# The v projection of the first 128 rows taken from un-normalised rows laid out by feature, with four matmuls on a tile of ones during the first loads

## The chip, the cores and the metric

The kernel runs on one core of one Trainium2 chip. A core has five engines that each work through a list of their own in order: TensorE for matmuls (PE in the profile; PEld is its loading of weights), VectorE (DVE), ScalarE (ACT), GpSimd (POOL) and SyncE (SP), which here issues the DMA transfers. They meet at semaphores. The metric is the device time of one launch in microseconds (us); lower is better. One profiled execution also leaves a trace, in which every instruction has a start and a duration.

## The reference

The reference is one inference step of a four-layer streaming encoder in float32. 640 rows of width 1024 go through it: 512 of a new stream and 128 of running streams. The change touches only the beginning of the first layer:

```python
def rms_norm(x, g):
    y = xf * lax.rsqrt(jnp.mean(xf * xf, axis=-1, keepdims=True) + EPS)
    return (y * g.astype(jnp.float32)).astype(x.dtype)
...
def chunk_mlp(u, v, v_gain, w_s, b_s):
    mu = jnp.mean(vf, axis=-1, keepdims=True)
    var = jnp.mean(jnp.square(vf - mu), axis=-1, keepdims=True)
    vn = ((vf - mu) * lax.rsqrt(var + EPS) * v_gain.astype(jnp.float32)).astype(v.dtype)
...
hp = rms_norm(xp, norm_mix_pre[layer])
proj = h @ w_in
u, v, bg, cg, xb = jnp.split(proj, ...)
```

A row `h` is `x * r * g`, where `r` is one number for the row and `g` one number for each feature. `v` is a product of `h` with 512 columns of `w_in`, and is then normalised over its 512 columns again.

## The kernel before

The 640 rows are five tiles of 128 rows (`t` = 0 to 4). The head of the program, up to the first units of the even mixer, does this:

- `main` queues the loads on SP's list: row tile 0, the gain `X.gain` (one row of 1024 numbers sent to all partitions), two of the four weight pieces of the v projection, row tile 1, the other two pieces. Row tiles 2 to 4 follow later. Every one of these transfers is 512 KB.
- `pre_norm` makes the norm of a row tile: ACT squares and sums it, DVE adds EPS, POOL takes the power -0.5 (the helper `rsqrt`), and DVE multiplies row, `r` and gain in one instruction. PE then transposes the tile in eight 128x128 steps into two PSUM banks (the helper `flip`), and `X.take` splits the result.
- A split (the helper `split`) writes a float32 value as a high part, made by ACT, and a low part, made by DVE as the difference. A product then takes three matmuls: high by high, high by low, low by high. The four weight pieces are split in the same way by `operand`.
- `Quarters` holds the transposed rows for later in seven tiles `x` (tag X), two tiles `a21` and two float32 copies `f`. `take` writes the splits (`x_93`, `x_94` and so on in the lists below) and copies of both banks to `f`. The tiles `a21` and `f` come from the pool `hidp`, which has seven buffers.
- `v_proj` makes 24 matmuls of 128x512 for each row tile: eight steps `k` over the features, three matmuls each, into one PSUM bank. `v_evac` then takes mean and variance of the bank on DVE, a power -0.5 on POOL, and writes the normalised tile `vn` on ACT. Three more `hidp` tiles hold `vn`.
- PSUM has eight banks, shared by transposes and products through the pool `psp`. A bank is free again when its last reader is done.
- The units of the mixer follow (`Units`, products of 128x320 from x and q tiles).

The order is set in two steps. `Weave` runs the generators against a clock of its own, which counts the matmuls issued; `pre_norm` of tile `t` is spawned with a wait of `A1 + (t - 1) * A2`, here 2000 and 5000. The Tile framework then arranges the instructions of each engine; `tc.high_priority()` moves the norms ahead, and while `Ordered.on` is set, ACT and DVE keep the program's order. What comes out is a fixed list for each engine.

Of the kernel before, what the change touches and what calls it, by code (L numbers as in the profile page):

```python
# [8 lines left out]
F32 = mybir.dt.float32  # L9
F32R = mybir.dt.float32r  # L10
AF = mybir.ActivationFunctionType
ALU = mybir.AluOpType
AX = mybir.AxisListType

P = 128
D = 1024
NK = D // P
# [8 lines left out]
HK = NK // 2  # L26
FT = 22
EPS = 1e-6
# [7 lines left out]
A1 = 2000  # L36
A2 = 5000
# [68 lines left out]
def trunk_kernel(  # L106
# [26 lines left out]
    c_w,  # L133
    c_scale,
    rb_rev,
    yp,
    ys,
    ncp,
# [9 lines left out]
    nc = tc.nc  # L148
    act, dve = Ordered(tc, nc.scalar), Ordered(tc, nc.vector)

    cst = ctx.enter_context(tc.tile_pool(name="cst", bufs=1))
# [3 lines left out]
    hidp = ctx.enter_context(tc.tile_pool(name="hidp", bufs=7))  # L155
# [6 lines left out]
    W = Weave()  # L162
# [6 lines left out]
    def flip(out, in_):  # L169
        W.now += 109  # L170
        nc.tensor.transpose(out=out, in_=in_, identity=ident)  # L171
# [3 lines left out]
    def nm(s):  # L175
        uid[0] += 1
        return f"{s}{uid[0]}"

    def bank(shape=(P, 512)):
        return psp.tile(list(shape), F32, tag="ps", name=nm("ps"))  # L180

    def t4(shape):
        return t4p.tile(list(shape), F32, tag="t4", name=nm("t4_"))

    def t2(shape):
        return t2p.tile(list(shape), F32, tag="t2", name=nm("t2_"))

    def st(n=1):
        return stp.tile([P, n], F32, tag="st", name=nm("st"))
# [8 lines left out]
    def bcast(src, n, alloc):  # L198
        g = alloc([P, n])
        nc.sync.dma_start(out=g, in_=src.partition_broadcast(P))  # L200
        return g

    def x10(shape, dtype=F32):
        return xpool.tile(list(shape), dtype, tag="X", name=nm("x"))

# [13 lines left out]
    def operand(src):  # L219
        n = src.shape[-1]  # L220
        q = qp.tile([P, 2, D], F32R, tag="q", name=nm("q"))
        split((q[:, 0, :n], q[:, 1, :n]), src)
        return q
# [4 lines left out]
    def split(dst, val):  # L228
        act.copy(out=dst[0], in_=val)
        dve.tensor_tensor(out=dst[1], in0=val, in1=dst[0].bitcast(F32), op=ALU.subtract)  # L230

    def rsqrt(ms):
        r = st()
        nc.gpsimd.tensor_tensor(out=r, in0=ms, in1=mhalf, op=ALU.pow)  # L234
        return r
# [113 lines left out]
                split((self.s4[:, 0, :, o], self.s4[:, 1, :, o]), s4)  # L349
                W.signal(self.sum[t], 4500)  # L350

    def pre_norm(t, x, X, wait, xn=None):
        if xn is None:
            xn = t4([P, D])
        with tc.high_priority():
            norm = Norm()
            norm.add(x, xn)
            r = norm.get()
            dve.scalar_tensor_tensor(out=xn, in0=x, scalar=r, in1=X.gain, op0=ALU.mult, op1=ALU.mult)
        yield wait  # L360
        ps = []
        for half in range(2):
            ps.append(bank((P, HK, P)))
            for i in range(HK):
                k = HK * half + i
                flip(ps[half][:, i, :], xn[:, k * P : (k + 1) * P])
        yield 500
        X.take(t, ps)

# [29 lines left out]
    def group_cols(g):  # L399
        return slice(0, GA) if g == 0 else slice(GA, NT)  # L400

    def wst(X, hl, g):
        for t in ((0, 1), (2, 3, 4))[g]:
            yield X.ev[t]
        cols = group_cols(g)
# [9 lines left out]
                yield  # L415
        return ps[:, :n]

    def v_proj(X, hls, evac):
        for t in range(TT):
            for e in X.ready(t):  # L420
                yield e
            ps = bank()
            for k in range(NK):
                q = hls[k // 2][:, :, k % 2 * 512 : (k % 2 + 1) * 512]
                x = X.rows(k, t)
                mm(ps, x[0], q[:, 0, :], k == 0, False, 512)
                mm(ps, x[0], q[:, 1, :], False, False, 512)
                mm(ps, x[1], q[:, 0, :], False, k == NK - 1, 512)
                if k % 4 == 3:
                    yield  # L430
            evac(t, ps)
# [50 lines left out]
    def in_row(t):  # L482
        return xp[t * P : (t + 1) * P, :] if t < 4 else xs
# [224 lines left out]
        o = hist_n + NP  # L708
        return buf[:, o : o + NB * (hist_n + LS)].rearrange("p (b s) -> p b s", s=hist_n + LS)

    def even_mixer(X, hls):
        vn = {}
        vns = [hidp.tile([P, 2, NT], F32, tag="hid", name=nm("vn")) for _ in range(3)]
        consts = [t4([P, 2, 512]) for _ in range(2)]
# [2 lines left out]
        def v_evac(t, ps):  # L717
            stats = st(6)
            dve.bn_stats(out=stats, in_=ps)
            mv = st(2)  # L720
            dve.bn_aggr(out=mv, in_=stats)
            ve = st()
            dve.tensor_scalar(out=ve, in0=mv[:, 1:2], scalar1=EPS, scalar2=None, op0=ALU.add)
            r = rsqrt(ve)
            vn[t] = vns[t // 2][:, t % 2, :512]
            nm_ = st()
            dve.scalar_tensor_tensor(
                out=nm_, in0=mv[:, 0:1], scalar=-1.0, in1=r, op0=ALU.mult, op1=ALU.mult
            )
            act.activation(out=vn[t], in_=ps, func=AF.Identity, scale=r, bias=nm_)  # L730
            if t == 4:
                o = t2([P, 512])
                dve.tensor_tensor(out=o, in0=vn[t], in1=gn, op=ALU.mult)
                nc.sync.dma_start(out=nav, in_=o)
# [1 line left out]
        gn = bcast(v_gain[0], 512, lambda _: consts[0][:, 0, :])  # L736
        gcol = cst.tile([P, 4], F32, name="gcol")
        nc.sync.dma_start(out=gcol, in_=v_gain_t)
        yield from v_proj(X, hls, v_evac)
        W.signal(v_ready, 4000)  # L740

        wT = consts[1][:, 0, :].rearrange("p (g i) -> p g i", i=P)
# [3 lines left out]
        for b in range(NB):  # L746
            r = slice(b * LS, (b + 1) * LS)
            nc.sync.dma_start(out=wS[r, :, r], in_=sp_wT[0:LS, :, 0:LS])
        for g in range(4):
            for w in (wT, wS):  # L750
                nc.gpsimd.affine_select(  # L751
                    out=w[:, g, :],
                    in_=w[:, g, :],
# [510 lines left out]
    def main():  # L1264
        X = Quarters(None, True)
        feed = fetch([ev_v[i] for i in range(4)])
        xt = []

        def load(t):
            xt.append(t4([P, D]))  # L1270
            nc.sync.dma_start(out=xt[t], in_=in_row(t))

        def start(t, wait):
            g = pre_norm(t, xt[t], X, wait)
            next(g)
            W.spawn(g, 0, wait)

        Ordered.on = True
        load(0)
        X.gain = bcast(g_mix_pre[0], D, t4)  # L1280
        w = [next(feed) for _ in range(2)]
        load(1)
        w += [next(feed) for _ in range(2)]
        first = pre_norm(0, xt[0], X, 0)
        next(first)
        hls = [operand(w[0])]
        for _ in first:
            pass
        W.signal(X.top[0])
        hls.append(operand(w[1]))  # L1290
        start(1, A1)
        hls += [operand(w[2]), operand(w[3])]
        for t in range(2, TT):
            load(t)
            start(t, A1 + (t - 1) * A2)
        Ordered.on = False
        X = yield from even_mixer(X, hls)
        nxt = []

        def mid():  # L1300
            gpost = bcast(g_ffn_post[0], D, t4)
            nxt.append(Normed(bcast(g_mix_pre[1], D, t4)))
            return make_fin(gpost, x_row, x_row, nxt[0])

        yield from ffn(0, X, mid)
        X = yield from odd_mixer(nxt[0])

        def end():
            gpost = bcast(g_ffn_post[1], D, t4)
            return make_fin(gpost, x_row, y_row, None)  # L1310

        yield from ffn(1, X, end)
# [97 lines left out]
```

## Time and profile before

| | |
|---|---|
| median of 3 runs | 1320.55 us (1320.53 to 1320.88) |
| the profiled execution: its time | 1320.24 us |
| its span, first to last instruction | 1318.5 us |
| DVE busy | 889.0 us (67%) |
| ACT busy | 614.0 us (47%) |
| POOL busy | 54.9 us (4%) |
| matmuls recorded | 8060 |
| moved by DMA | 150.12 MB, mean 114 GB/s |

Times in a timeline are counted from the span's start. A timeline's row has the start, the busy time, the engine, the source line, the operation with its output and input tiles and their shape, the number of instructions merged into the row, and in brackets the idle time ahead of it with what ended that. Helpers record many operations, so many rows carry line 99 (the wrapper around ACT and DVE) or 167 (the helper `mm`), and the tile names tell them apart.

### The profile page before, as it was taken

Reading aid. Unit: us, or ns where it says so; the run is one execution under the profiler, and the core shown is the slowest. Engines: PE = TensorE matmul, PEld = TensorE weight load, DVE = VectorE, ACT = ScalarE, POOL = GpSimd, SP = SyncE. Lnnn points to the kernel's source line nnn. Section 1 sums busy time; section 2 is a strip of 40 time slices with the busy share of each in tenths; the row PEclk is TensorE's granted clock in tenths of the full one; section 3 lists DMA queues with packets and bytes.
Section 4 is the critical chain, followed back from the end, with each engine's and each line's share of the span. In section 5 each row is a group of like instructions: output and inputs, shape, how many; then the busy total and the mean of one; then the engine's idle time right before and its main releaser. Section 6 shows DMA issues by size and latency. Waiting matters only on the chain.

```text
span 1318.5 us, 20069 instructions
## 1 busy us (share of the span) xinstructions
PE 1294.0 (98%) x8060; PEld 1178.4 (89%) x8060; DVE 889.0 (67%) x1452; ACT 614.0 (47%) x1130; POOL 54.9 (4%) x107
## 2 busy tenths in 40 slices
PE   6999999999999999999999999999999999999997
PEld 5998989989899998998799885789999898998996
DVE  6985779837576675776736556489557575864766
ACT  5644546535254352454433455366455261551551
POOL 2200101000000000000210000010000000000000
PEclk9999999999999999999999999999999999999999
DMA  7212253212223122126435336532213021230233
GB/s 249 73 65 81 96 200 138 96 48 81 96 73 120 53 77 112 64 84 218 163 120 195 147 143 250 197 128 102 107 64 128 32 98 63 96 115 30 97 128 128
DMA packets 45965, 150.12 MB, mean 114 GB/s; under 512 B 6576, under 2 KB 8496, under 8 KB 45872
## 3 DMA queue, kind: packets, MB, share of 16 engines
q1 hardware_dynamic: 45872, 148.84, 31.2%
q8 instruction: 63, 1.03, 0.3%
q14 instruction: 30, 0.25, 0.1%
HBM read 133.57 MB, written 15.26 MB: 113 GB/s over the span
## 4 chain that ended last, share of the span: by engine, by line
PE 86%; DVE 5%; issue 3%; ACT 2%; DMA 2%; POOL 1%; SPq 0%; DVEq 0%; POOLq 0%; ACTq 0%
PE ps L167 84%; DVE t L99 3%; PE ps L171 1%; DMA xbuf<-t 1%; POOL st L234 1%; ACT t L99 1%; DMA raw<-in_dram 1%; DVE q L99 1%; ACT q L99 1%; DVE x L99 1%; DVE st L99 0%; ACT ps L99 0%; ACT f L99 0%; POOL t L751 0%; SPq L380 0%
## 5 line engine op out<-in xcount | busy, mean ns | idle before, releaser
L167 PE MATMUL ps<-x,q 128*128 128x320 f32 (+2 forms) x4884 | 727.4, 309 | 1.2 <-DVE q L99 0.8
L167 PEld LDWEIGHTS ps<-x,q 128*128 128x128 f32 x4884 | 717.5, 188 | 6.2 <-issue 2.9
L167 PE MATMUL ps<-q,hid 128*128 128x512 f32 x1800 | 417.3, 391 | 0.2 <-DVE hid L99 0.2
L99 ACT CAST q<-raw 128x1024 fp32r<-128x1024 f32 (+1 forms) x278 | 269.7, 977 | 296.8 <-PE ps L167 247.1
L99 DVE TENSOR_TENSOR q<-raw,q 128x1024 fp32r<-128x1024 f32 (+1 forms) x278 | 313.9, 1132 | 134.4 <-ACT q L99 129.3
L167 PEld LDWEIGHTS ps<-q,hid 128*128 128x128 f32 x1800 | 335.5, 188 | 70.9 <-issue 1.7
L99 ACT COPY t<-ps 128x320 f32<-128x320 f32 (+2 forms) x304 | 135.0, 451 | 193.7 <-PE ps L167 173.8
L99 DVE TENSOR_TENSOR t<-ps,t 128x512 f32<-128x512 f32 (+2 forms) x164 | 100.3, 614 | 93.2 <-PE ps L167 93.0
L99 DVE TENSOR_TENSOR raw<-raw 128x512 f32<-128x512 f32 (+1 forms) x141 | 121.9, 866 | 11.6 <-DMA raw<-in_dram 10.0
L99 DVE TENSOR_TENSOR t<-t,t 128x512 f32<-128x512 f32 (+4 forms) x107 | 57.8, 551 | 48.5 <-ACT t L99 46.7
L234 POOL TENSOR_TENSOR st<-st,mhalf 128x1 f32<-128x1 f32 x45 | 31.7, 705 | 1005.9 <-DVE st L99 1001.1
L99 DVE SCALAR_TENSOR_TENSOR t<-t,st,t 128x512 f32<-128x512 f32 (+1 forms) x60 | 54.5, 925 | 16.6 <-POOL st L234 15.1
L99 ACT ACTIVATE t<-t 128x320 f32<-128x320 f32 (+1 forms) x60 | 40.1, 668 | 45.0 <-issue 26.2
L171 PE MATMUL ps<-ident,t 128*128 128x128 f32 x288 | 42.2, 281 | 12.0 <-DVE t L99 9.6
L171 PEld LDWEIGHTS ps<-ident,t 128*128 128x128 f32 x288 | 33.4, 143 | 21.9 <-DVE t L99 9.9
L99 ACT CAST hid<-t 128x320 fp32r<-128x320 f32 (+1 forms) x96 | 45.9, 482 | 11.1 <-DVE t L99 8.9
L99 DVE TENSOR_TENSOR t<-t 128x320 f32<-128x320 f32 (+3 forms) x90 | 48.8, 542 | 1.4
L99 DVE TENSOR_TENSOR hid<-t,hid 128x320 fp32r<-128x320 f32 (+1 forms) x96 | 48.8, 512 | 0.1
L167 PE MATMUL ps<-q,x 128*128 128x512 f32 x192 | 47.6, 402 | 1.2 <-DVE st L99 0.8
L99 ACT ACTIVATE ps<-t 128x512 f32<-128x512 f32 x40 | 24.1, 603 | 50.6 <-DVE t L99 50.6
L167 PEld LDWEIGHTS ps<-q,x 128*128 128x128 f32 x192 | 36.1, 192 | 10.6 <-DVE q L99 2.3
L99 DVE TENSOR_TENSOR t<-t,ps 128x320 f32<-128x320 f32 x47 | 22.9, 487 | 33.2 <-PE ps L167 33.2
(90 smaller groups left out, 497.5 us busy)
## 6 DMA issues: line engine op xcount, KB each, us to landing
raw<-in_dram SPq DMA_DIRECT2D x184, 512.0 KB, 4.1
x<-in_dram SPq DMA_DIRECT2D x24, 512.0 KB, 6.1
t<-in_dram SPq DMA_DIRECT2D x22, 512.0 KB, 5.8
xbuf<-t SPq DMA_DIRECT2D x15, 512.0 KB, 3.4
t<-xbuf SPq DMA_DIRECT2D x15, 512.0 KB, 3.9
out_dram<-t SPq DMA_DIRECT2D x15, 256.0 KB, 2.0
c<-in_dram SPq DMA_DIRECT2D x4, 512.0 KB, 4.2
fscr<-x SPq DMA_DIRECT2D x2, 768.0 KB, 3.3
```

The source lines that it names most:

```text
L99: ins = op(*args, **kw)
L167: nc.tensor.matmul(out, lhsT=lhsT, rhs=rhs, start=start, stop=stop, skip_group_check=more)
L171: nc.tensor.transpose(out=out, in_=in_, identity=ident)
L234: nc.gpsimd.tensor_tensor(out=r, in0=ms, in1=mhalf, op=ALU.pow)
```

## The change

Row tile 0 is loaded twice. The host lays out the first 128 rows by feature (`first_t`: 128 features, eight groups, 128 rows), and the gain in the same way (`first_g`). Two loads of 256 KB bring `first_t`; DVE multiplies the first half by the gain and POOL the second; ACT and DVE split the halves into two new `hidp` tiles `top`. The v projection of tile 0 takes these, and so does not wait for tile 0's norm. The factor `r` of the row, which it lacks, is put in afterwards: `v_evac` of tile 0 multiplies the variance by `r` twice and the scale by `r` once (two more instructions of 128x1). The row-wise tile 0 is still loaded, normed, transposed and kept, for the units.

The order of the loads becomes: first half of `first_t`, `first_g`, two weight pieces, second half of `first_t`, row tile 1, two weight pieces, the gain row, row tile 0. Tile 1 is normed ahead of tile 0, and the waits of the spawns are new. Ahead of all this DVE writes a tile of ones, and four float32 matmuls of 128x512 multiply it by itself into a bank that nobody reads.

```diff
-    def pre_norm(t, x, X, wait, xn=None):
+    def pre_norm(t, x, X, wait, xn=None, scale=None, pause=False):
...
             r = norm.get()
+            if scale is not None:
+                scale.append(r)
+        if pause:
+            yield
+        with tc.high_priority():
             dve.scalar_tensor_tensor(out=xn, in0=x, scalar=r, in1=X.gain, op0=ALU.mult, op1=ALU.mult)
...
-    def v_proj(X, hls, evac):
+    def v_proj(X, hls, evac, first=None):
         for t in range(TT):
-            for e in X.ready(t):
-                yield e
+            if t or first is None:
+                for e in X.ready(t):
+                    yield e
...
+                    x = [f[:, k, :] for f in first]
...
+            var = mv[:, 1:2]
+            if t == 0:
+                var = st()
+                dve.tensor_scalar(
+                    out=var, in0=mv[:, 1:2], scalar1=scale[0], scalar2=scale[0], op0=ALU.mult, op1=ALU.mult
+                )
             ve = st()
-            dve.tensor_scalar(out=ve, in0=mv[:, 1:2], scalar1=EPS, scalar2=None, op0=ALU.add)
+            dve.tensor_scalar(out=ve, in0=var, scalar1=EPS, scalar2=None, op0=ALU.add)
             r = rsqrt(ve)
+            if t == 0:
+                own, r = r, st()
+                dve.tensor_tensor(out=r, in0=own, in1=scale[0], op=ALU.mult)
...
-        load(0)
-        X.gain = bcast(g_mix_pre[0], D, t4)
-        w = [next(feed) for _ in range(2)]
+        ones = t2([P, 512])
+        dve.memset(ones, 1.0)
+        ps = bank()
+        for _ in range(4):
+            nc.tensor.matmul(ps, lhsT=ones[:, :P], rhs=ones, start=True, stop=True)
+        gt = cst.tile([P, NK], F32, name="gt")
+        xt0 = t4([P, NK, P])
+        nc.sync.dma_start(out=xt0[:, :HK], in_=first_t[:, :HK])
+        nc.sync.dma_start(out=gt, in_=first_g)
+        w = [next(feed)]
+        nc.sync.dma_start(out=xt0[:, HK:], in_=first_t[:, HK:])
+        w.append(next(feed))
+        xt.append(None)
         load(1)
         w += [next(feed) for _ in range(2)]
-        first = pre_norm(0, xt[0], X, 0)
+        X.gain = bcast(g_mix_pre[0], D, t4)
+        xt[0] = t4([P, D])
+        nc.sync.dma_start(out=xt[0], in_=in_row(0))
+        top = [hidp.tile([P, NK, P], F32R, tag="hid", name=nm("top")) for _ in range(2)]
+        hls = []
+        for i in range(2):
+            c = slice(i * HK, (i + 1) * HK)
+            (nc.gpsimd if i else dve).tensor_tensor(
+                out=xt0[:, c], in0=xt0[:, c], in1=gt[:, c].unsqueeze(2).broadcast_to([P, HK, P]), op=ALU.mult
+            )
+        for i in range(2):
+            c = slice(i * HK, (i + 1) * HK)
+            split((top[0][:, c], top[1][:, c]), xt0[:, c])
+            hls.append(operand(w[i]))
+        second = pre_norm(1, xt[1], X, A1 + 3000, pause=True)
+        next(second)
+        hls += [operand(w[2]), operand(w[3])]
+        next(second)
+        W.spawn(second, 0, A1 + 3000)
+        scale = []
+        first = pre_norm(0, xt[0], X, 0, None, scale)
         next(first)
...
+        W.spawn(first, 0, 2 * A2 - 500)
         for t in range(2, TT):
             load(t)
-            start(t, A1 + (t - 1) * A2)
+            start(t, A1 + t * A2 - 500)
```

The change moves instructions on all engines in the head. Three places are shown: PE and ACT from the end of row tile 1's v projection to the start of tile 2's, and DVE where the units' first weights are split. The lists name a tile with its number; `[waits ...]` names the engines or DMA queues whose semaphore a row waits for.

On PE before, `ps_291` is the v product of row tile 1, `ps_316` and `ps_321` the transposes of row tile 3, and `ps_337` the v product of row tile 2 (its transposed rows are in `q_92`):

```order
L167 MATMUL ps_291<-q_154,x_94 128x512 x3
L167 MATMUL ps_291<-q_157,x_94 128x512 x6
L171 MATMUL ps_316<-ident,t_38_172 128x128 [waits DVE_49,PE_49]
L171 MATMUL ps_316<-ident,t_38_172 128x128 x3
L171 MATMUL ps_321<-ident,t_38_172 128x128 [waits PE_49]
L171 MATMUL ps_321<-ident,t_38_172 128x128 x3
L167 MATMUL ps_337<-q_124,q_92 128x512 [waits Activation_49]
L167 MATMUL ps_337<-q_124,q_92 128x512 x5
```

On PE now, `ps_258` is the v product of row tile 1, `ps_281` and `ps_286` the transposes of row tile 2, `ps_351` and `ps_356` those of row tile 3, and `ps_382` the v product of row tile 2:

```order
L173 MATMUL ps_281<-ident,t_36_166 128x128 x3
L173 MATMUL ps_286<-ident,t_36_166 128x128 [waits PE_49]
L173 MATMUL ps_286<-ident,t_36_166 128x128 x3
L169 MATMUL ps_258<-q_149,x_94 128x512 x5
L169 MATMUL ps_258<-q_152,x_94 128x512 x6
L173 MATMUL ps_351<-ident,t_41_176 128x128 [waits Activation_49]
L173 MATMUL ps_351<-ident,t_41_176 128x128 x3
L173 MATMUL ps_356<-ident,t_41_176 128x128 [waits PE_49,Activation_49]
L173 MATMUL ps_356<-ident,t_41_176 128x128 x3
L169 MATMUL ps_382<-q_134,q_92 128x512 [waits PE_49,Activation_49]
```

The transposes of tile 3 now wait for ACT, where before they waited for DVE and PE, and tile 2's v product stands behind them.

On ACT before, `vn_190<-ps_198` is the normalised v of row tile 0, and the copies to `f_102` and `f_103` empty the banks of the transposed tiles 0 to 2 (`ps_211`/`ps_216` is tile 1, `ps_250`/`ps_255` tile 2; those of tile 0 stand further ahead):

```order
L99 COPY f_102<-ps_211 128x4x128 [waits DVE_49]
L99 CAST q_92<-ps_250 128x512 [waits PE_49]
L99 COPY f_103<-ps_216 128x4x128 [waits DVE_49]
L99 ACTIVATE t_38_172,st_173<-t_37_170 128x1024 [waits DMAHW6_49]
L99 CAST q_92<-ps_255 128x512 [waits PE_49]
L99 CAST x_93<-ps_250 128x4x64 [waits DVE_49]
L99 CAST x_94<-ps_255 128x4x64 [waits DVE_49]
L99 COPY f_102<-ps_250 128x4x64 [waits DVE_49]
L99 ACTIVATE t_43_182,st_183<-t_42_180 128x1024 [waits DMAHW1_49]
L99 COPY f_103<-ps_255 128x4x64 [waits DVE_49]
```

On ACT now, `vn_194<-ps_202` is the normalised v of row tile 0, `t_41` the square of row tile 3 and `t_46` that of row tile 4; the copies to `f` are those of tile 1 (`ps_227`/`ps_232`), tile 0 (`ps_271`/`ps_276`) and tile 2:

```order
L99 CAST q_92<-ps_286 128x512 [waits PE_49]
L99 ACTIVATE t_41_176,st_177<-t_40_174 128x1024 [waits DMAHW1_49,DVE_49]
L99 CAST x_93<-ps_281 128x4x64 [waits DVE_49]
L99 CAST x_94<-ps_286 128x4x64 [waits DVE_49]
L99 ACTIVATE t_46_186,st_187<-t_45_184 128x1024 [waits DMAHW4_49]
L99 ACTIVATE vn_194<-ps_202,st_249,st_247 128x512 [waits DVE_49]
L99 COPY f_102<-ps_227 128x4x128
L99 COPY f_103<-ps_232 128x4x128
L99 COPY f_102<-ps_271 128x4x128
L99 COPY f_103<-ps_276 128x4x128
```

All copies to `f` now stand behind the normalised v of tile 0, where before each stood behind its own tile's splits.

On DVE before, `q_528<-raw_525` is the low part of the units' first weights, `st_416` the variance of the v product of tile 2, and `x_96` to `x_99`, `t_82` to `t_84` belong to the sums that `take` makes of row tile 3 (`t_78`, `x_99`) and of row tile 4 (from `t_82` on):

```order
L99 TENSOR_TENSOR t_78_358<-t_77_357,f_103 128x512
L99 BN_AGGR st_416<-st_414 128x2
L99 TENSOR_TENSOR q_528<-raw_525,q_528 128x1024 [waits DMAHW4_49]
L99 TENSOR_TENSOR x_99<-t_78_358,x_99 128x4x128 [waits Activation_49]
L99 TENSOR_TENSOR t_82_399<-ps_376,t_81_397 128x512
```

On DVE now, `q_552<-raw_549` is that low part, `st_476` the variance of the v product of tile 3, and `t_95` to `t_97` and `x_96` to `x_98` belong to the sums of row tile 4:

```order
L99 TENSOR_TENSOR t_96_448<-t_95_447,f_102 128x512 [waits DVE_49]
L99 TENSOR_TENSOR t_94_445<-f_102,t_94_445 128x512
L99 TENSOR_TENSOR x_96<-t_95_447,x_96 128x4x128 [waits Activation_49]
L99 TENSOR_TENSOR x_97<-t_96_448,x_97 128x4x128 [waits Activation_49]
L99 TENSOR_TENSOR x_98<-t_94_445,x_98 128x4x128 [waits Activation_49]
L99 TENSOR_TENSOR t_97_449<-t_96_448,f_103 128x512
L99 BN_AGGR st_476<-st_474 128x2
L99 TENSOR_TENSOR q_552<-raw_549,q_552 128x1024 [waits DMAHW5_49]
```

The low part now stands behind the sums of tile 4, where before it stood ahead of them.

More of the change, by code (lines that the diff above doesn't have):

```diff
@@ L135, in trunk_kernel @@
     rb_rev,
+    first_t,
+    first_g,
     yp,
@@ L424, in v_proj @@
                 q = hls[k // 2][:, :, k % 2 * 512 : (k % 2 + 1) * 512]
-                x = X.rows(k, t)
+                if t or first is None:
+                    x = X.rows(k, t)
+                else:
+                    x = [f[:, k, :] for f in first]
                 mm(ps, x[0], q[:, 0, :], k == 0, False, 512)
@@ L709, in seg, with even_mixer @@
         return buf[:, o : o + NB * (hist_n + LS)].rearrange("p (b s) -> p b s", s=hist_n + LS)
-    def even_mixer(X, hls):
+    def even_mixer(X, hls, first, scale):
         vn = {}
@@ L738, in even_mixer @@
         nc.sync.dma_start(out=gcol, in_=v_gain_t)
-        yield from v_proj(X, hls, v_evac)
+        yield from v_proj(X, hls, v_evac, first)
         W.signal(v_ready, 4000)
@@ L1278, in main @@
         Ordered.on = True
-        load(0)
-        X.gain = bcast(g_mix_pre[0], D, t4)
-        w = [next(feed) for _ in range(2)]
+        ones = t2([P, 512])
[11 more added lines that the diff above has]
+        xt.append(None)
         load(1)
         w += [next(feed) for _ in range(2)]
-        first = pre_norm(0, xt[0], X, 0)
-        next(first)
[L1286 to L1292, printed above, removed]
+        X.gain = bcast(g_mix_pre[0], D, t4)
[19 more added lines that the diff above has]
+        first = pre_norm(0, xt[0], X, 0, None, scale)
+        next(first)
+        W.spawn(first, 0, 2 * A2 - 500)
         for t in range(2, TT):
             load(t)
-            start(t, A1 + (t - 1) * A2)
+            start(t, A1 + t * A2 - 500)
         Ordered.on = False
-        X = yield from even_mixer(X, hls)
+        X = yield from even_mixer(X, hls, top, scale)
         nxt = []
@@ L1382 @@
         i["d_rel_bias"][:, :, ::-1],
+        i["x_prompt"][0, :P].reshape(P, NK, P).transpose(2, 1, 0),
+        i["norm_mix_pre"][0].reshape(NK, P).T,
     ]
```

## The prediction

> **What bounds the kernel now.** The page comes first: busy shares, and the chain of work that ended last.
>
> ```profile
> span 1318.5 us, 20069 instructions
> PE 1294.0 (98%) x8060; PEld 1178.4 (89%) x8060; DVE 889.0 (67%) x1452; ACT 614.0 (47%) x1130; POOL 54.9 (4%) x107
> ...
> PE 86%; DVE 5%; issue 3%; ACT 2%; DMA 2%; POOL 1%; SPq 0%; DVEq 0%; POOLq 0%; ACTq 0%
> ```
>
> PE sets the time: whatever delays its list by a microsecond costs one. The windows by stage show where it is not full.
>
> ```profile
> 0.00:10.00 10.00, 1.96 (x9) 1.74 (x9) 2.67 (x4) 4.06 (x5) 1.38 (x9) 1.00 0.80 281
> ...
> 400.00:600.00 200.00, 200.00 (x1218) 189.44 (x1218) 131.84 (x182) 86.57 (x143) 0.00 (x0) 1.00 0.26 92
> ```
>
> The columns are PE, PEld, DVE, ACT, POOL busy, clock, DMA share and GB/s. The start is the weak place, and the change is all there. PE's own timeline of it:
>
> ```profile
> 8.04 1.97 PE L171 MATMUL ps<-ident,t 128*128 128x128 f32 x8 [8.04 <-DVE t L99]
> 9.83 3.04 PE L167 MATMUL ps<-q,x 128*128 128x512 f32 x6
> 13.06 0.50 PE L167 MATMUL ps<-q,x 128*128 128x512 f32 x1 [0.19 <-ACT q L99]
> 14.32 1.64 PE L167 MATMUL ps<-q,x 128*128 128x512 f32 x6 [0.76 <-DVE st L99]
> ...
> 17.48 2.79 PE L167 MATMUL ps<-q,x 128*128 128x512 f32 x11
> 20.62 1.09 PE L171 MATMUL ps<-ident,t 128*128 128x128 f32 x8 [0.36 <-DVE t L99]
> 21.47 5.71 PE L167 MATMUL ps<-q,x 128*128 128x512 f32 x24
> 27.03 1.03 PE L171 MATMUL ps<-ident,t 128*128 128x128 f32 x8
> 27.82 2.98 PE L167 MATMUL ps<-q,q 128*128 128x512 f32 x12
> ...
> 32.31 0.66 PE L171 MATMUL ps<-ident,t 128*128 128x128 f32 x4 [0.38 <-ACT vn L99]
> ...
> 34.89 2.89 PE L167 MATMUL ps<-q,a 128*128 128x512 f32 x12
> 37.61 2.88 PE L167 MATMUL ps<-q,x 128*128 128x512 f32 x12
> ...
> 45.77 7.20 PE L167 MATMUL ps<-x,q 128*128 128x320 f32 x48
> ```
>
> Tile 0's v product runs piecemeal from 9.83, tile 1's 24 matmuls begin at 21.47, tile 2's at 27.82, and at 45.77 the units begin. Early matmuls take 0.50 us each, later ones 0.227 (2.72 from 34.89 to 37.61 for twelve); transposes 0.246 at 8.04 and 0.11 at 20.62. The granted clock stays 1.00 in the windows, so this slowness after the idle start is seen in the durations alone. At 32.31 PE waited 0.38 us for ACT's `vn`: tile 4's transposes needed a bank. That small wait is what the change makes large.
>
> **The change part by part.** Times below are read off the new lists, step by step, with durations of the trace. First, when does row tile 0 arrive?
>
> ```profile
> 2.00:3.00 1.00, 0.00 (x0) 0.00 (x0) 0.00 (x0) 0.09 (x1) 0.00 (x0) 1.00 0.92 356
> 3.00:4.00 1.00, 0.00 (x0) 0.00 (x0) 0.00 (x0) 0.00 (x0) 0.00 (x0) 1.00 1.06 344
> ...
> 13.00:14.00 1.00, 0.50 (x1) 0.19 (x1) 0.96 (x1) 1.00 (x4) 0.00 (x0) 1.00 0.63 250
> ```
> ```profile
> 4.11 1.06 ACT L99 ACTIVATE t<-t 128x1024 f32<-128x1024 f32 x1 [2.03 <-DMA t<-in_dram]
> 5.60 0.55 POOL L234 TENSOR_TENSOR st<-st,mhalf 128x1 f32<-128x1 f32 x1 [4.14 <-DVE st L99]
> 6.70 1.28 DVE L99 SCALAR_TENSOR_TENSOR t<-t,st,t 128x1024 f32<-128x1024 f32 x1 [1.26 <-DMA t<-in_dram]
> ...
> 7.94 1.05 ACT L99 CAST q<-raw 128x1024 fp32r<-128x1024 f32 x1 [2.68 <-DMA raw<-in_dram]
> 9.02 1.23 DVE L99 TENSOR_TENSOR q<-raw,q 128x1024 fp32r<-128x1024 f32 x1 [1.04 <-ACT q L99]
> 9.22 0.33 SPq L1271 DMA_DIRECT2D t<-in_dram  x1
> ...
> 14.30 0.33 SPq L214 DMA_DIRECT2D raw<-in_dram  x1
> ```
>
> Before, row tile 0 was the first load and ACT began on it at 4.11. The eighth 512 KB load was issued at 9.22, the ninth at 14.30, and in the window from 13 the DMA moves 250 KB where full windows move some 400, so it falls still at about 13.7: eight loads take until then. Now two halves, four weights, tile 1 and the gain go ahead of row tile 0, which is the eighth load: 13.7, plus 0.7 (the first 0.52 MB was through at 3.4, ACT began at 4.11), **14.4**.
>
> The rest is priced by these rows of the timeline, and the warm-up by one group of instructions with kept shapes (busy us, mean ns):
>
> ```profile
> 17.04 1.07 ACT L99 CAST x<-ps 128x512 fp32r<-128x512 f32 x2
> 18.54 0.68 DVE L99 TENSOR_TENSOR x<-ps,x 128x512 fp32r<-128x512 f32 x1
> ...
> 24.20 0.53 POOL L745 MEMSET t<- 128x512 f32 x1
> 24.28 1.28 DVE L99 SCALAR_TENSOR_TENSOR t<-t,st,t 128x1024 f32<-128x1024 f32 x1 [0.66 <-POOL st L234]
> ...
> 26.09 0.41 DVE L99 TENSOR_TENSOR x<-ps,x 128x256 fp32r<-128x256 f32 x1
> ...
> 28.73 2.01 POOL L751 TENSOR_SCALAR_AFFINE_SELECT t<-t 128x128 f32<-128x128 f32 x4
> ...
> 31.48 0.78 ACT L99 ACTIVATE vn<-ps,st,st 128x512 f32<-128x512 f32 x1 [2.51 <-DVE st L99]
> ```
> ```profile
> L167 PE MATMUL ps<-t,x 128*128 128x512 f32 x8 | 4.2, 606 | 0.0
> ```
>
> And PE's widest gap behind the start, from its timeline, with the longest piece of the chain that follows the head:
>
> ```profile
> 829.01 1.30 PE L167 MATMUL ps<-x,t 128*32 128x128 f32 x40 [1.38 <-ACT t L99]
> ```
> ```profile
> 221.62 386.72 PE ps L167 x2343
> ...
> 608.36 0.72 DVE t L99 x2
> ```
>
> *What it removes.* Tile 0's product no longer waits for the norm and the transposes; it follows the splits. By the same byte rates half A, the first weights and half B land near 3.5, 5.3 and 7.2. ACT has half B's high part behind POOL's multiplication (7.2 + 1.2 = 8.4), then 0.6 for that, 1.05 for weights two, 1.3 for the square of tile 1 with its sum (5.4 from 4.11), 2.1 for the other weights: 13.4, and DVE 1.23 for the last low part: 14.6. Five matmuls on, tile 0's product ends at **15.8**, not 20.3 (17.48 + 2.79).
>
> The multiplication on POOL is not in the trace: 0.53 (a memset of that size) bounds it from below, 2.0 (four selects over as many elements) from above. I take 1.2, the middle; the upper end adds 0.7, since ACT's list waits for it, the lower takes off nothing, as tile 0's norm then decides. By the Trainium skill ("GPSIMD Engine Reference", "4.1 Engine selection") a two-input operation is about twice as slow there as on VectorE, an estimate of 1.4 with DVE's 0.68, and no run here shows it; the sum would be 0.2 higher.
>
> The four warm-up products are covered by PE's idle first 8 us. Float32 instructions of 128x512 take 0.53 each on a fast array (4.2 / 8), and at 0.50 for 0.227 about 1.2 on a slow one; at one or two instructions each the four end between 5 and 11. Tile 0's first low part is split at 7.6, so up to 3 could be uncovered, but its product waits for splits until 14.6 and has that much slack: nothing.
>
> The added splits, casts and DVE's 0.68 are in ACT's and DVE's lists as walked here.
>
> *What then runs late.*
>
> 1. Tile 0's norm from 14.4: 2.04 to the power's end (4.11 to 6.15), then 1.28 on DVE: 17.7.
> 2. PE: three transposes of tile 0, then tile 1's product, whose low part is split on DVE behind that multiplication (0.68, at 18.54 before): 18.4. Ten matmuls, 2.3: 20.7. Five more transposes: 21.3.
> 3. ACT meanwhile has tile 0's high parts ahead of everything else: 20.9 plus 1.07, then two of tile 2, 1.07: 23.0. Behind them the square of row tile 3, and 2.04 more to its multiplication on DVE: **25.1**. Before, that stood at 24.28.
> 4. From there to the end of tile 0's `vn` it took 7.98 (24.28 to 32.26). One 512-wide subtraction less stands in between (-0.6), and two new 128x1 operations (+0.3): **32.8**.
> 5. PE: one matmul, tile 2's transposes, eleven matmuls: tile 1's product is done at **24.9**. Next are tile 3's transposes, which wait for ACT. All eight banks are held: tile 0's v, tile 1's v, and two each for the transposes of tiles 1, 0 and 2. The copies to `f` that would free them have no buffers in their pool of seven (two `top`, two `a21`, two `f`, three `vn` make nine), and stand behind `vn` on ACT. So PE idles from 24.9 to 32.8, **7.9 us**, with tile 2's product queued behind.
> 6. Eight transposes, 0.87: tile 2's product starts at 33.7 instead of 27.82, +5.9. To the units: three products of 5.44 and eight transposes, 17.2, where it was 17.95: 50.9 instead of 45.77, **+5.1**.
> 7. The clock. No row shows a gap like this in mid-kernel: no gap behind 15 us exceeds the 1.38 above, and that one's matmuls are fast; matmuls after the idle 8.04 at the start are slow for seven. The ends are 0 and, by the start's rows, 8 x 0.137 + 7 x 0.27 = 3.0. 7.9 is near 8.04: I take **+3.0**, and PE reaches the units at 53.9. The Trainium skill ("TensorE: Matmul & The Clock Gate", "What's actually happening") gives the array half its clock after an idle window of 3.4 us and full clock after one busy window; by that the loss is an estimate of 1.7, and the sum 1.3 lower. The trace's start, slow from 9.83 to past 13.56, agrees with the rule in kind and is longer.
> 8. DVE's first low part for the units:
>
> ```profile
> 39.14 0.68 DVE L99 TENSOR_TENSOR t<-t,f 128x512 f32<-128x512 f32 x1
> 39.74 0.68 DVE L99 TENSOR_TENSOR t<-f,t 128x512 f32<-128x512 f32 x1
> ```
>
> It now stands behind tile 4's sums. From 31.9 there are 22 operations of 512 at 0.6 (39.14 to 39.74), ten of 256 at 0.33 (0.41 with the same overlap of 0.08), nine small at 0.1, two POOL steps at 0.6, itself 1.2, and waits for ACT of up to 2: 51.7 to 53.8. PE, at 53.9 with ten matmuls to do first, does not notice; without step 7 it would arrive at 50.9 and lose up to 1.4.
>
> Sum: 5.1 + 3.0 = **+8.1**. Later lists are alike, and the lag stays: PE alone carries the chain from 221 to 608, and the pause there starts when its last products are done. 1320.24 (the profiled run; the median of the runs is 0.3 higher) + 8.1 = **1328.3 us**.
>
> **The rivals.**
>
> *Not slower: the bank comes in time.* If tile 0's `vn`, or another reader, freed a bank early, tile 3's transposes would wait only for their own rows, 26.4 (25.1 + 1.28 on DVE). Tile 2's product would start at 27.3, 0.5 ahead of before, 17.2 instead of 17.95 would follow, and the gap of 1.5 is near the harmless one, so the clock stays: -1.3, 1318.9, give or take 1. For it: the product of tile 0 is done at 15.8, so `vn` could be early. Against: DVE's list has its statistics behind the multiplication of tile 3, and ACT's list has it behind the square of tile 4. It decides from the point where `vn` ends by 26.4, 6.4 us before step 4 has it.
>
> *About the same: half the wait.* Every microsecond by which row tile 0 lands earlier, or ACT's casts in step 3 run ahead, takes one off the gap. Four of them leave 1.1 on step 6 and a gap too near the harmless ones for step 7: 1321.3. Against: SP's order and the byte rate fix step 1 within about 1.
>
> *Slower, but the clock stays up:* 5.1 to 6.5, 1325.3 to 1326.7.
>
> *The warm-up does not do what it says.* If the ones leave PE slow, tile 0's product at 0.50 each ends at 19.6 (7.6 + 12), and tile 0's transposes, step 2 on, shift by some 2.5: 1330.8. Against: the four are long enough by the bounds above, and tile 0's product follows at once.
>
> **How the numbers follow.** A measurement of this kernel can tell about 0.2% (2.6 us) from no change. Chances: the forecast with its clock loss 0.60, its own range 1326 to 1330 (steps 1 and 4, POOL's bound); clock up 0.15; no warm-up 0.04; half the wait 0.09; the bank in time 0.12, of which half lies below 1317.9. That makes slower 0.79, same 0.15, faster 0.06. The range 1321 to 1331 leaves out the last case (0.12), a part of half the wait and a rest above (0.04 each).
>
> **What would show it.** In the changed profile: row tile 0's square on ACT near 14.4; PE without work from about 25 to 33, ended by ACT `vn`; transposes of 0.25 and matmuls of 0.5 behind it; the units near 54. A square of tile 0 before 12, a `vn` before 26, or PE busy through 25 to 33 would make the forecast wrong; fast matmuls behind the gap would strike step 7 alone.

## The result and the profile after the change

| | before | after |
|---|---|---|
| median | 1320.62 us (1320.53 to 1320.88, 4 runs) | 1332.20 us (1331.16 to 1334.39, 4 runs) |
| ratio | | 1.0089 (95% interval 1.0074 to 1.0104) |
| the profiled execution: its time, its span | 1320.24, 1318.5 us | 1333.09, 1331.4 us |
| mean granted clock of TensorE (1 is full speed) | 0.999 | 0.992 to 0.996 |

The change costs 11.6 us. The prediction had 1328.3 us and 1321 to 1331: the sign is right, the time is 3.9 us higher than forecast, and it lies 1.2 us above the range. The page of the changed kernel begins:

```profile
span 1331.4 us, 20122 instructions
...
PE 1302.9 (98%) x8068; PEld 1182.5 (89%) x8068; DVE 893.3 (67%) x1458; ACT 614.7 (46%) x1132; POOL 56.3 (4%) x108
...
PE 85%; DVE 5%; issue 3%; DMA 3%; POOL 2%; ACT 1%; SPq 0%; DVEq 0%; POOLq 0%; ACTq 0%
```

The shares hardly differ; nothing in them shows where 13 us went. TensorE's timeline of the head does (start, busy, operation, count, idle time ahead and what ended it):

```profile
1.52 6.25 PE L1304 MATMUL ps<-t 128*128 128x512 f32 x8 [1.52 <-DVE t L99]
...
12.84 5.75 PE L169 MATMUL ps<-q,top 128*128 128x512 f32 x17 [0.77 <-DVE st L99]
...
35.07 1.97 PE L173 MATMUL ps<-ident,t 128*128 128x128 f32 x8 [7.83 <-ACT vn L99]
36.69 7.67 PE L169 MATMUL ps<-q,q 128*128 128x512 f32 x24
44.19 1.03 PE L173 MATMUL ps<-ident,t 128*128 128x128 f32 x8
...
55.96 0.74 PE L169 MATMUL ps<-x,q 128*128 128x320 f32 x4
```

The first row is the ones. Tile 0's product ends at 18.59 (12.84 + 5.75); the forecast had 15.8, and 20.27 was the time before. The gap stands in front of tile 3's transposes, 7.83 us, ended by ACT's `vn`, and the slow matmuls stand behind it. The units begin at 55.96 instead of 45.77. The windows now show the granted clock falling, which it did nowhere in the head before (last three columns: clock, DMA share, GB/s):

```profile
14.00:15.00 1.00, 1.00 (x3) 0.58 (x3) 1.00 (x2) 0.47 (x1) 0.00 (x0) 0.50 1.12 220
...
30.00:31.00 1.00, 0.00 (x0) 0.00 (x0) 1.00 (x3) 0.00 (x0) 0.29 (x1) 0.79 0.06 5
31.00:32.00 1.00, 0.00 (x0) 0.00 (x0) 0.94 (x2) 0.00 (x0) 1.00 (x3) 0.50 0.09 8
...
40.00:41.00 1.00, 1.00 (x5) 0.77 (x4) 1.00 (x4) 0.44 (x2) 0.00 (x0) 0.59 0.00 0
41.00:42.00 1.00, 1.00 (x6) 0.83 (x5) 1.00 (x3) 1.00 (x4) 0.00 (x0) 1.00 0.00 0
```

ACT's timeline has row tile 0's square, its `vn`, and the copies to `f` right behind it:

```profile
15.38 1.06 ACT L99 ACTIVATE t<-t 128x1024 f32<-128x1024 f32 x1 [0.91 <-DMA t<-in_dram]
...
34.24 0.78 ACT L99 ACTIVATE vn<-ps,st,st 128x512 f32<-128x512 f32 x1 [6.21 <-DVE st L99]
34.91 2.31 ACT L99 COPY f<-ps 128x512 f32<-128x512 f32 x5
```

How the lag grows along the program is read from the chain of work at the same steps: first of before, then of after.

```profile
176.01 1.92 PE ps L167 x7
...
896.94 407.79 PE ps L167 x2436
```
```profile
186.22 1.92 PE ps L169 x7
...
233.22 386.72 PE ps L169 x2343
...
909.93 407.81 PE ps L169 x2436
```

With 221.62 of before, the lag is 10.2 us at the first step, 11.6 at the second and 13.0 at the third. So 2.8 us are lost far behind the edit, where the forecast had nothing.

### The profile page after: what moved, and what is told of

Read it like the earlier page. It is cut to its first block, busy times and chain, and to the rows that moved or that the text cites. A ratio compares the mean times of both kernels' runs of the same rounds, so it can differ in the third digit from the quotient of the medians.

```text
span 1331.4 us, 20122 instructions
## 1 busy us (share of the span) xinstructions
PE 1302.9 (98%) x8068; PEld 1182.5 (89%) x8068; DVE 893.3 (67%) x1458; ACT 614.7 (46%) x1132; POOL 56.3 (4%) x108
## 4 chain that ended last, share of the span: by engine, by line
PE 85%; DVE 5%; issue 3%; DMA 3%; POOL 2%; ACT 1%; SPq 0%; DVEq 0%; POOLq 0%; ACTq 0%
PE ps L169 84%; DVE t L99 4%; PE ps L173 2%; POOL st L236 1%; DMA xbuf<-t 1%; ACT t L99 1%; DMA t<-in_dram 1%; DMA raw<-in_dram 1%; DVE q L99 1%; DVE st L99 0%; DVE x L99 0%; DMA x<-in_dram 0%; ACT q L99 0%; ACT ps L99 0%; ACT x L99 0%
## 5 line engine op out<-in xcount | busy, mean ns | idle before, releaser
L169 PE MATMUL ps<-q,x 128*128 128x512 f32 x168 | 40.7, 394 | 0.9 <-DVE q L99 0.7
L99 ACT ACTIVATE t<-ps,st 128x512 f32<-128x512 f32 (+4 forms) x48 | 24.5, 513 | 37.0 <-DVE st L99 31.9
```

Of the source, the lines that this page charges most:

```text
L99: ins = op(*args, **kw)
L169: nc.tensor.matmul(out, lhsT=lhsT, rhs=rhs, start=start, stop=stop, skip_group_check=more)
```

## The experiments

All compute the full result; the products with zeros add nothing to a sum. Ratios are to the kernel before on the same chip. The experiments ran on different chips, on which the kernel before has medians of 1320.79 to 1321.23 us; where two of them differ by little, the ratios are given beside the medians.

**Why the banks come late: too few buffers, or the order of their use?** The prediction said that the copies to `f` have no room (nine tiles for seven buffers). One kernel keeps the nine tiles and only uses `f` and `a21` once ahead of everything:

```diff
+        for x in X.f + [a.bitcast(F32) for a in X.a21]:
+            nc.gpsimd.memset(x[:, 0, :1], 0.0)
         hls = []
```

> The changed kernel with four one-column memsets on POOL that write the two f and the two a21 tiles once, in the program's order ahead of the first vn. Theory A (the pool hands its buffers out in the order in which the program first uses the tiles, and the first vn stands ahead of f in that order): the copies to f run ahead of vn, the 7.8 us gap ahead of row tile 3's transposes shrinks to the wait for that tile's own norm (some 2 us), no slow stretch follows, and the time is 1322 to 1325 us. Theory B (as predicted: nine tiles for seven buffers, so the copies have no room until vn is done): the count is the same, the gap stays, 1331 to 1334 us.

The other makes seven tiles of the nine:

```diff
-        top = [hidp.tile([P, NK, P], F32R, tag="hid", name=nm("top")) for _ in range(2)]
+        top = [t4p.tile([P, NK, P], F32R, tag="t4", name=nm("top")) for _ in range(2)]
```

> The changed kernel with the two tiles top taken from the pool t4p instead of hidp, so that hidp has seven tiles for seven buffers as before the change. Theory B (too few buffers): the copies to f have room, the gap ahead of row tile 3's transposes is gone, 1322 to 1325 us. Theory A (order of first use): the gap stays at 5 to 8 us, 1330 to 1334 us.

The early use gives 1328.07 us (1327.25 to 1329.01), ratio 1.0053 (1.0040 to 1.0065); seven tiles give 1333.86 us (1332.87 to 1334.27), ratio 1.0095 (1.0081 to 1.0109). The first transposes behind the gap, on TensorE's timeline, with the early use and then with seven tiles:

```profile
29.41 1.94 PE L173 MATMUL ps<-ident,t 128*128 128x128 f32 x8 [2.46 <-DVE t L99]
31.01 6.36 PE L169 MATMUL ps<-q,q 128*128 128x512 f32 x24
```
```profile
35.10 1.97 PE L173 MATMUL ps<-ident,t 128*128 128x128 f32 x8 [5.71 <-ACT vn L99]
```

With room for all, the transposes still wait for `vn`; with four tiny writes and the same count, they wait only for their own norm. That bears out theory A: the pool hands out buffers in the order in which the program first uses the tiles. (Which of `f` and `a21` had to be early was not tried apart.) Tile 0's product no longer waits for anything, so its `vn` had moved ahead of the first copy to `f` in that order. The time is still above what was expected of the early use (1322 to 1325 us): that counted neither the later 2.8 us nor the slow stretch, which this kernel still has behind 2.46 us of idling.

**Does the slow stretch come from the gap, and is it worth its 3 us?** Zero products fill the gap:

```diff
...
+            if t == 1 and first is not None:
+                for i in range(30):
+                    nc.tensor.matmul(ps, lhsT=zero, rhs=q[:, 0, :], start=False, stop=i == 30 - 1)
             evac(t, ps)
```

> The changed kernel with 30 products with a tile of zeros (128x512, float32r) added to row tile 1's v product, so that TensorE works through most of the gap. If the slow matmuls behind the gap come from TensorE being idle in it: products at 0.23 us and a granted clock of 1.00 there, 3 us less, 1328 to 1330 us. If they come from something else (the load on the chip, the time since the start): the same 1331 to 1334 us, with half clock at the same place.

Measured 1332.59 us (1332.05 to 1333.36), ratio 1.0086 (1.0073 to 1.0100): no gain, although the granted clock now stays at 1.00 from 16 to 46 us. So the slow stretch does come from the gap. TensorE's timeline of this kernel, and a row of its DVE:

```profile
26.18 7.16 PE L445 MATMUL ps<-q,zero 128*128 128x512 f32 x30
34.18 1.13 PE L173 MATMUL ps<-ident,t 128*128 128x128 f32 x8 [0.83 <-ACT vn L99]
35.14 5.75 PE L169 MATMUL ps<-q,q 128*128 128x512 f32 x24
...
56.00 6.71 PE L169 MATMUL ps<-x,q 128*128 128x320 f32 x44 [1.48 <-DVE st L99]
```
```profile
54.75 1.20 DVE L99 TENSOR_TENSOR q<-raw,q 128x1024 fp32r<-128x1024 f32 x1
```

From the transposes behind the gap to the next ones it takes 9.12 us in the changed kernel (35.07 to 44.19), and 6.55 here. But TensorE then stands still for 1.48 us at 56.00, until DVE has made the low part of the units' first weights (54.75 + 1.20 = 55.95; the row names another small tile of DVE's at that moment). In the changed kernel that row is here, and before the change it was there:

```profile
56.02 1.19 DVE L99 TENSOR_TENSOR q<-raw,q 128x1024 fp32r<-128x1024 f32 x1
```
```profile
42.84 1.19 DVE L99 TENSOR_TENSOR q<-raw,q 128x1024 fp32r<-128x1024 f32 x1
```

It is done at 57.21, just when TensorE, slow or not, has its first ten unit matmuls behind it. Two bounds end together. So both were taken away, with the zero products and a high priority for that one split:

```diff
...
-            self.cols = [unit(feed) for _ in range(2)]
+            self.cols = []
+            for _ in range(2):
+                src = next(feed)
+                if early_q:
+                    early_q.pop()
+                    with tc.high_priority():
+                        self.cols.append(operand(src))
+                else:
+                    self.cols.append(operand(src))
```

> The run with the 30 zero products in the gap, and besides it the split of the units' first weights given high priority, so that DVE makes their low part ahead of row tile 4's sums (some 43 us instead of 54.75 to 55.95). Theory A (two bounds end together near 56 us, TensorE with its half clock and DVE with that low part, so that taking away one alone gains nothing): both away, TensorE comes to the units 2 to 3 us earlier, 1329 to 1330.6 us. Theory B (what the restored clock gained was lost in something else, such as the added products): 1332 to 1333 us as with the zero products alone.

Measured 1330.88 us (1330.63 to 1331.72), ratio 1.0078 (1.0064 to 1.0092). DVE makes the low part at 41.90, TensorE has no idle stretch between 35 and 62 us, and the time is 1.7 us below that with the zero products alone by the medians, 1.1 by the ratios, whose intervals overlap. In the two profiled executions the chain's long last step begins at 909.45 and 908.01, 1.4 us apart. The direction is theory A's; the median is 0.3 us short of the gain that was expected.

```profile
41.90 1.22 DVE L99 TENSOR_TENSOR q<-raw,q 128x1024 fp32r<-128x1024 f32 x1
```

**What the ones do.** Without the tile of ones and its four matmuls in the changed kernel, and with them in the kernel before:

```diff
-        ones = t2([P, 512])
-        dve.memset(ones, 1.0)
-        ps = bank()
-        for _ in range(4):
-            nc.tensor.matmul(ps, lhsT=ones[:, :P], rhs=ones, start=True, stop=True)
```

> The changed kernel without the tile of ones and its four matmuls. If the ones do nothing for row tile 0's v product (its first half waits for splits, and the granted clock falls to 0.50 behind them anyway): 1331 to 1334 us. If they keep its matmuls fast up to 13 us, the product without them ends 1 to 3 us later and the time is 1333 to 1336 us.

> The kernel before with the tile of ones and its four matmuls, and nothing else of the change. Theory A (they warm the array, and the first transposes and products run at full clock): transposes of 0.11 us, tile 0's product still bound by its splits, 0 to 1 us faster than before, 1320.2 to 1321.2 us. Theory B (thin work behind the ones lowers the clock again, as in the changed kernel): a half-clock stretch at 12 to 16 us, 1321 to 1322.5 us.

1332.45 us (1331.37 to 1332.99), ratio 1.0085 (1.0071 to 1.0098), and 1321.18 us (1320.39 to 1322.01, 11 runs), ratio 1.0001 (0.9992 to 1.0010): the ones are worth nothing that can be measured in either. In the kernel before they do make the first eight transposes fast (1.09 us where it was 1.97), as theory A has it, and the stretch of half clock behind them is theory B's. TensorE's timeline of the changed kernel without them:

```profile
6.72 0.80 PE L169 MATMUL ps<-q,top 128*128 128x512 f32 x1 [6.72 <-ACT q L99]
7.98 3.28 PE L169 MATMUL ps<-q,top 128*128 128x512 f32 x6 [0.46 <-DVE q L99]
11.73 1.64 PE L169 MATMUL ps<-q,top 128*128 128x512 f32 x6 [0.47 <-DVE q L99]
13.72 2.79 PE L169 MATMUL ps<-q,top 128*128 128x512 f32 x11 [0.35 <-DVE q L99]
```

The first seven are slow, the rest fast, and the product ends at 16.51. With the ones the first six are fast, then the work is thin (it waits for splits), and the clock falls to 0.50 while it goes on. The earlier end is not all due to that: half B came to POOL at 7.72 in this execution and at 8.89 in that of the changed kernel. Counted from there the product ends 8.8 us later without the ones, 9.7 in the changed kernel, and 8.7 in the kernel with one block (below), which has the ones and whose clock stayed up there (8.27 to 17.01). So the fall costs some 1.0 us, and without it the ones make no difference. The kernel before with the ones shows the same fall, by its windows:

```profile
14.00:16.00 2.00, 1.84 (x4) 1.50 (x5) 1.33 (x3) 2.00 (x3) 0.55 (x1) 0.50 0.34 102
```

To see what this fall costs, ten zero products keep TensorE busy there (three behind the first matmul of k = 0 and of k = 2, four behind k = 1):

```diff
                 mm(ps, x[0], q[:, 0, :], k == 0, False, 512)
+                if t == 0 and first is not None and k in {0: 3, 2: 3}:
+                    for _ in range({0: 3, 2: 3}[k]):
+                        nc.tensor.matmul(ps, lhsT=zero, rhs=q[:, 0, :], start=False, stop=False)
...
+                if t == 0 and first is not None and k in {1: 4}:
+                    for _ in range({1: 4}[k]):
+                        nc.tensor.matmul(ps, lhsT=zero, rhs=q[:, 0, :], start=False, stop=False)
```

> The changed kernel with ten products with a tile of zeros put between the first matmuls of row tile 0's v product, so that TensorE is busy from 7 to 13 us. Theory A (the granted clock falls to 0.50 from 12 to 16 us because TensorE has little to do before): the clock stays at 1.00, the product ends near 17.0 instead of 18.0 to 18.6 us, and the time falls by 0.5 to 1.5 us, 1330.7 to 1331.7. Theory B (row tile 0's landing and DVE's multiplication of it decide the next steps anyway): the product ends earlier, but the time stays at 1332 to 1333 us.

Measured 1332.30 us (1330.97 to 1332.54), ratio 1.0086 (1.0072 to 1.0100). The clock stays at 1.00 from 12 to 16 us and the product ends at 17.81, 8.8 us after half B came to POOL (8.97), but nothing is gained that can be measured: theory B, for the changed kernel. With the early use besides:

> The early use of f and a21 and the ten zero products in row tile 0's v product together. If the two losses add up: 0.5 to 1.5 us less than with the early use alone (1328.07 us), so 1326.5 to 1327.6 us. If row tile 0's landing decides in between: 1327.6 to 1328.6 us. Either way slower than before, since the later lists of the changed kernels lose 1.4 us between 180 and 228 us and as much again by 905 us, as all four runs so far did.

Measured 1326.77 us (1325.24 to 1327.31), ratio 1.0042 (1.0030 to 1.0055): 1.3 us less than with the early use alone by the medians, 1.5 by the ratios, whose intervals overlap. The number is that of losses that add up; where it comes from is not shown. The slow stretch behind the shorter gap goes too in this kernel's profile, though TensorE idles as long in front of it (2.47 us): tile 3's transposes and tile 2's product take 6.4 us (28.63 to 35.01) instead of 7.8 (29.41 to 37.20), and these 1.4 us are most of the 2.0 between the two profiled executions.

**Where the later 2.8 us come from.** One such place, on TensorE before and after:

```profile
214.14 3.78 PE L167 MATMUL ps<-x,q 128*128 128x320 f32 x24 [0.43 <-DVE q L99]
```
```profile
225.75 3.78 PE L169 MATMUL ps<-x,q 128*128 128x320 f32 x24 [1.47 <-DVE q L99]
```

TensorE waits 1.04 us longer for a low part of weights on DVE. DVE's own rows there, before and after:

```profile
208.81 0.68 DVE L99 TENSOR_TENSOR t<-t,t 128x512 f32<-128x512 f32 x1
209.40 1.28 DVE L99 SCALAR_TENSOR_TENSOR t<-t,st,t 128x1024 f32<-128x1024 f32 x1
...
212.87 1.22 DVE L99 TENSOR_TENSOR q<-raw,q 128x1024 fp32r<-128x1024 f32 x1
```
```profile
220.68 1.28 DVE L99 SCALAR_TENSOR_TENSOR t<-t,st,t 128x1024 f32<-128x1024 f32 x1 [0.40 <-POOL st L236]
...
222.54 1.28 DVE L99 TENSOR_TENSOR t<-t,t 128x512 f32<-128x512 f32 x2
...
224.48 1.22 DVE L99 TENSOR_TENSOR q<-raw,q 128x1024 fp32r<-128x1024 f32 x1
```

Before, a multiplication of 512 columns filled the time in which POOL takes the power. Now the norm's multiplication comes first, DVE idles 0.40 us for POOL, and two 512-wide ones follow in front of the weights. The code of that stage is the same in both but for one helper: `pre_norm` serves every later norm too, and the diff closes its high-priority block ahead of that multiplication and opens a second one, so that one caller can pause in between. Put back for all callers but that one:

```diff
             if scale is not None:
                 scale.append(r)
+            if not pause:
+                dve.scalar_tensor_tensor(out=xn, in0=x, scalar=r, in1=X.gain, op0=ALU.mult, op1=ALU.mult)
         if pause:
             yield
-        with tc.high_priority():
-            dve.scalar_tensor_tensor(out=xn, in0=x, scalar=r, in1=X.gain, op0=ALU.mult, op1=ALU.mult)
+            with tc.high_priority():
+                dve.scalar_tensor_tensor(out=xn, in0=x, scalar=r, in1=X.gain, op0=ALU.mult, op1=ALU.mult)
```

> The changed kernel with the multiplication in pre_norm put back into the same high-priority block as the square ahead of it, for all norms but row tile 1's first. Theory A (the split of that block in the shared helper reorders DVE's lists in the later norm stages, and that costs the 1.4 us between 186 and 233 us and the 1.4 between 620 and 910): the head keeps its loss, the two later losses are gone, 1329 to 1330 us. Theory B (the later losses come from the head being late, or from the extra tiles): 1332 to 1333 us.

And the split alone, in the kernel before (one more `with tc.high_priority():` in front of that multiplication):

> The kernel before with that block split in two and nothing else. Theory A: the head is as before, and 2.4 to 3 us are lost in the later norm stages, 1323.2 to 1323.9 us. Theory B: as before, 1320.5 to 1321.3 us.

1329.60 us (1328.77 to 1330.77), ratio 1.0064 (1.0052 to 1.0077), against 1332.20; and 1323.42 us (1322.80 to 1324.42, 11 runs), ratio 1.0017 (1.0008 to 1.0026), against 1321.01. Both are theory A's. The place on TensorE in the changed kernel with one block, and in the kernel before with two:

```profile
222.60 3.79 PE L169 MATMUL ps<-x,q 128*128 128x320 f32 x24 [0.43 <-DVE q L99]
```
```profile
215.60 3.78 PE L167 MATMUL ps<-x,q 128*128 128x320 f32 x24 [1.47 <-DVE q L99]
```

The chain of the changed kernel with one block has the three steps at

```profile
184.29 1.92 PE ps L169 x7
...
230.08 386.72 PE ps L169 x2343
...
905.59 407.80 PE ps L169 x2436
```

a lag of 8.3, 8.5 and 8.7 us: the head alone, and then it nearly stays. It grows by 0.4 us instead of 2.8, and that is the block's worth; the 1.9 us less at the first step are the head's, where the clock did not fall behind the ones in this execution. The kernel before with two blocks has no such difference in its head, and there the lag is 0.1, 1.5 and 2.8 us:

```profile
176.09 1.90 PE ps L167 x7
...
223.08 386.71 PE ps L167 x2343
...
899.76 407.79 PE ps L167 x2436
```

**All three mends together:**

> All three mends together: f and a21 used early, ten zero products in row tile 0's v product, the block in one piece. If they add up: 1326.77 less 2.4 to 3 us, 1323.7 to 1324.4 us, still 0.2 to 0.3% slower than before, by the two idle stretches of 2.5 and 0.6 us that TensorE has left at row tile 3's norm and tile 4's v product.

Measured 1323.33 us (1322.46 to 1326.56, 11 runs), ratio 1.0020 (1.0011 to 1.0029): 3.4 us below the two mends without it by the medians, 2.9 by the ratios, where 2.4 to 3 were expected. What is left is 2.3 us. In the profiled execution the lag at the three steps of the chain is 3.0, 3.2 and 3.2 us, so nearly all of it is in the head. TensorE's timeline shows two idle stretches for it, at tile 3's transposes (which wait for row tile 3's norm) and at tile 4's product:

```profile
28.98 1.06 PE L173 MATMUL ps<-ident,t 128*128 128x128 f32 x8 [2.47 <-DVE t L99]
...
46.43 2.56 PE L169 MATMUL ps<-q,a 128*128 128x512 f32 x10 [0.60 <-DVE a L99]
```

That these two are what is left is argued, not tested. No version beats the kernel before.

## Why the prediction was wrong, by its own steps

- **The step that failed is the last one: "Later lists are alike, and the lag stays".** It put the later loss at nothing, and was taken from the chain, not from the lists. DVE's lists differ in the later norm stages, because the diff splits the priority block of a shared helper. That costs 2.6 us (1332.20 to 1329.60; 3.3 by the two ratios, whose intervals just overlap; 2.4 by the growth of the lag) and, alone in the kernel before, 2.4. With the block mended the changed kernel stands 8.6 us behind the kernel before; the prediction's sum for the head was 8.1. The rest of the 3.9 us is this 0.5, 0.4 from the profiled execution to the median of before, and the spread of the runs.
- **Tile 0's product and steps 1 to 4 came late.** Row tile 0's square began at 15.38 instead of 14.4 in the profiled execution, at 14.79 in the one without the ones, at 15.74 in the one with ten zero products: the landing moves by 1 us between executions. Tile 0's product ended at 18.59 instead of 15.8: half B came to POOL at 8.89 instead of 7.2, the last low part was done at 15.9 instead of 14.6, and the clock was down to 0.50 in the window from 14. The prediction took the array to stay fast from the ones on, which was wrong in this execution. Step 4 came at 35.02 instead of 32.8, and the units at 55.96 instead of 53.9. In the kernel with one block, whose clock did not fall there, the square began at 14.78, the product ended at 17.01, step 4 came at 33.70 and the units at 54.13: so of the 2.1 us that the head lagged beyond the forecast in the profiled execution, 1.8 were not there in this one.
- **Step 5, the gap, was right in place and size** (7.83 us for 7.9, ended by `vn`), **and wrong in its cause.** The size is in part luck: both ends of the gap came 2.2 to 2.3 us late (27.24 for 24.9, 35.07 for 32.8). As for the cause, it is the order of first use and not the number of buffers: seven tiles in seven buffers leave the gap, four tiny writes remove it.
- **Step 7, the clock, was right in kind, and near in size in this execution:** the 8 transposes and 24 products behind the gap take 9.12 us, and 6.39 in the kernel with all three mends (28.98 to 35.37), so 2.7 for the forecast's 3.0. In the four other kernels with such a gap, one execution each, the loss was 1.8 to 2.9 (8.14 us with ten zero products, 9.27 with seven tiles). The Trainium skill ("TensorE: Matmul & The Clock Gate", "What's actually happening") has the clock halved after at least one idle window of 3.4 us and whole after at least one busy one; the prediction's estimate of 1.7 took one. Here TensorE stops at 27.24, the clock falls at 30.6 and is whole again at 40.8, 5.7 us after work resumed at 35.07; over these five executions it fell 2.1 to 5.0 us after the last matmul and came back 3.7 to 6.1 us after the next one. The return agrees with "at least one", and so 1.7 was a lower end; the fall does not always, since 2.1 us is less than one idle window.
- **Steps 7 and 8 were not to be added as they were.** The low part for the units was put at 51.7 to 53.8 and came at 57.2, beside TensorE. Where two engines end together, the term of one is not a gain to be had alone: filling the gap gave nothing, filling it and moving the low part 1.7 us (1.1 by the ratios).
- **The warm-up costs nothing, as forecast, but it brings nothing either.** The rival "does not do what it says" put the kernel with a slow product at 1330.8; without the ones the time is the same within noise (1332.45 for 1332.20). That rival's end of tile 0's product (19.6, measured 18.59) was near by luck: it had every matmul at 0.50, while the first six behind the ones were fast and those in a later window slow.

## What to carry to other kernels

A change in a shared helper is made at every call: compare the instruction lists of the whole program, not only those of the edited stage, since a priority block that is split in two moved DVE's order some 180 us behind the edit, and cost as much again further on. Where a product no longer has to wait, everything that it first uses moves ahead in the queue for buffers, and may shut out what the others wait for. And where a stall is removed, ask what ends second before counting the gain.

## What the runs showed of the hardware

- Matmuls behind the idle start are slow while the granted clock reads 1.00 (0.50 us each at 10 to 13 us before the change, 0.227 later), but slow stretches behind the ones or behind the gap do show in it as 0.50.
- The clock can also fall without a full stop: after seven fast matmuls in 5 us it read 0.50 for 3.4 us in the changed kernel and in the kernel before with ones. In two kernels with the same head (zero products and high priority; one block) it stayed at 1.00. In the same way 2.46 us without work lowered it in one kernel (early use) and 2.47 us left it whole in another, with the same work on TensorE in the 9 us ahead.
- Windows of 0.1 us show an order in this. Every stretch of low clock in the heads lasted 3.4, 6.8 or 10.2 us, that is one, two or three times 3.41. Where there are two, the second began four or five times 3.41 us after the first ended (16.92 to 30.58 in the changed kernel, 15.32 to 28.98 with the early use, 17.31 to 34.37 with seven tiles). So the clock seems to be set once in 3.41 us, on a grid that lies differently in each execution. In the 3.41 us ahead of each fall TensorE was busy for at most 1.9 us (1.55 in the changed kernel, 1.40 with the early use), though 1.85 us did not lower it in the kernel with seven tiles; in the kernel with one block, whose head has the same work, the two steps of the grid there had 2.33 us each, and the clock stayed up. That would explain why the same work slows down in one execution and not in the next; it is read off these traces and was not tested.
- A multiplication of 128x512 with a gain broadcast along the rows took POOL 1.04 us (1.12 at most in the other executions) and DVE 0.69, so 1.5 times as long; the forecast had taken 1.2 for POOL.

```profile
8.89 1.04 POOL L1322 TENSOR_TENSOR t<-t,gt 128x512 f32<-128x512 f32 x1 [7.43 <-DMA t<-in_dram]
```
